# First attention of a two-layer trunk: doubled key heads, five single PSUM banks, early rows by weight, a new list order, and SyncE in that order

## The chip, the cores and the metric

The kernel runs on one core of one Trainium2 chip. A core has TensorE (PE), VectorE (DVE), ScalarE (ACT), GpSimd (POOL) and SyncE (SP); here SP only issues DMA transfers. The metric is the device time of one execution in microseconds (us), the median of several runs.

## The reference, cut to what matters

The model is a two-layer decoder trunk on 1024 rows of 1024 numbers, all in fp32. The first layer is a forgetting attention with 16 heads of 64, and the change lies in it. A gated FFN with a convolution, a shared key/value side, a sparse attention and a second FFN follow.

```python
def forgetting_attention(xn, w_in, b_f, q_gain, k_gain, w_out):
    proj = xn @ w_in
    q = rms_norm(proj[..., :HD].reshape(B, T, N_HEADS, HEAD_DIM), q_gain)
    k = rms_norm(proj[..., HD:2 * HD].reshape(B, T, N_HEADS, HEAD_DIM), k_gain)
    v = proj[..., 2 * HD:3 * HD].reshape(B, T, N_HEADS, HEAD_DIM)
    log_f = jax.nn.log_sigmoid((proj[..., 3 * HD:] + b_f).astype(jnp.float32))
    c = jnp.cumsum(log_f, axis=1).transpose(0, 2, 1)
    ...
        s = jnp.einsum('bhqd,bhkd->bhqk', qb, k) * scale
        s = s + cb[..., :, None] - c[..., None, :]
        s = jnp.where(kpos[None, :] <= qpos[:, None], s, -jnp.inf)
        p = jax.nn.softmax(s, axis=-1)
        return jnp.einsum('bhqk,bhkd->bqhd', p, v)
    ...
    return o @ w_out
```

## The kernel before, in words

Each fp32 factor is split into a high and a low part ("hi" and "lo", names ending in `_h` and `_l`), and a product is three matmuls, hi by hi, lo by hi, hi by lo (L219 to L221). ACT rounds the high part, and DVE or POOL subtracts it to get the low part.

The first layer has three stretches. `fox_in` projects q, k and v in tiles of 128 rows, row-normalizes the heads and stores q and k, transposed and split, in DRAM (`s_q`, `s_k`), and v in `s_v`. The upper eight heads of rows 512 to 1023 are left out there. `fox_attn` is the attention: in units of one head and one half of the query rows, SP loads q, k and v of the unit (L801), PE forms the scores (L626) in a pair of PSUM banks (`s`), DVE adds the mask and takes the row maximum (L634), ACT takes the exponential (L636), DVE the reciprocal (L639), and POOL scales the rows (L640). Then `key_tasks` turns the weights, one key tile at a time: PE transposes up to four 128x128 blocks into a single bank `t` (L653), ACT and DVE split them (L664 `p_h`, L666 `p_l`), and PE multiplies with v (L658, L659) into the bank `v`. Beside the attention, PE does the projections left out by `fox_in` (`late_tasks`, whose sums lie in `t` banks too) and the output projection of rows 0 to 639 (`proj_tasks`). Their weights come from DRAM in quarters of 512 KB, `w_raw<-in_a_w_in` (L706) and `w_raw<-in_a_w_out` (L928), and are split by ACT (L893 `w_h`, `wo_h`) and POOL (L894).

The order in which the queues run is made while the program is built. A `Flow` holds tasks with an engine, an assumed duration, a priority (`u` plus a number by the task's letter from a table `PLAN`) and the buffers that they take and use. It walks through the list with assumed times: on each engine, the task that could start first is emitted, and among those that could, the one of lowest priority. A task that `takes` a buffer starts only when all tasks that `use` the last tenant of its room are done. `Trunk.run` (L210) then fixes the emitted order on PE, ACT, DVE and POOL. On SP it is not fixed: there the framework's own scheduler places the DMA issues. Each queue then runs in order, and an instruction that waits holds up all behind it on that queue.

In `key_tasks` the transposes have the v buffer of their unit among the buffers that they use. The products, which read that buffer, have not:

```python
        a = F.add("PE", .109 * len(blocks) - .09, u + 1 + x, "K", turn, after=after, takes=[t, p2], uses=uses)
        ...
        rooms["uses"] = [*rooms.get("uses", ()), p2, *then_uses]
        pv.tasks.append(F.add("PE", .035 + n / 1240 + (.5 if then else 0), u + 1 + x, "V", product, after=[l, *then_after, *pv.tasks[:1]], **rooms))
```

So for the list a v buffer is free with the last transposes of its unit. In the program, the load into it waits on a semaphore for the last product. There are four v buffers.

Of the kernel before, what the change touches and what calls it, by code (L numbers as in the profile page):

```python
# [50 lines left out]
def moved(*shape):  # L51
# [4 lines left out]
PLAN = {  # L56
    "fox": dict(F=1e3, G=-11.5, R=.5, M=5, E=-1, K=-.5, H=-1.5, L=-5.5, V=2, J=-4, D=1.5, N=18.5, Q=1.5, W=13, P=-3, S=0, O=1, spread=.7, wo=.6, wo_from=21, side=2, late=2, step=1.6, gap=.015),
    "ffn0": {"": 18.5, "A": -1.5, "B": -11, "C": -11, "D": -10, "I": 4.5, "P": -12, "R": 14.5, "S": -6, "T": 23, "U": 24, "V": 23, "W": -7, "a": -2.5, "b": -12, "c": 12, "d": -7, "e": -12, "f": -4, "g": -20, "h": -8, "l": 21, "n": 16.5, "r": -8, "s": -6, "t": -6, "x": 23.5, "y": 23.5},
    "ffn1": {"": 0, "A": 12.5, "B": -4, "C": -12, "D": 12.5, "I": 15.5, "P": -11.5, "R": 3.5, "S": 12, "T": 18, "U": 24, "V": 17, "W": 4.5, "a": -12, "b": 8, "c": -12, "d": -3, "f": 0.5, "l": 19.5, "n": -11, "s": 17.5, "t": -8},
    "nin": {"": 0},  # L60
    "nsa": dict(P=20.5, S=5.0, F=23.5, G=1000.0, R=4.5, M=12.0, E=20.0, D=-12, K=1.5, H=12.0, L=-10.0, V=20.0, J=14.0, O=22, N=19.0, Q=9.5, W=16.0, spread=0.3, wo=3, wo_from=2, side=2, cmp=0.5, gap=0.05),
}
# [39 lines left out]
class Flow:  # L102
# [14 lines left out]
    def add(self, eng, dur, u, kind, fn, after=(), takes=(), uses=()):  # L117
        t = Task(eng, dur + (self.plan.get("gap", 0) if eng == "PE" else 0), u + self.plan.get(kind, 0), fn, takes, (*takes, *uses))
# [77 lines left out]
class Trunk:  # L196
# [224 lines left out]
    def fox_in(self, cp, xT, qT, kT, vS, extras, room):  # L421
        nc, A = self.nc, self.A
        w_in = A["a_w_in"][0]
        with self.pool("fi_s", 2) as sp, self.pool("fi_w", 2) as wp, \
# [12 lines left out]
            def gate():  # L437
# [37 lines left out]
                for x, c in enumerate((ch, cl)):  # L475
                    nc.sync.dma_start(kT[:, :, 2 * HD + x, :].rearrange("p a t -> (p a) t"), f32(c))

            def spill(o, dst, half, i, gain):

                tl = slice(i * P, (i + 1) * P)  # L480
                ps = pp.tile([P, 4, P], FT, name="ps_t", tag="ps_t")
                for k in range(4):
                    nc.tensor.transpose(ps[:, k], o[:, k * P:(k + 1) * P], self.ident)
                hi = sp.tile([P, 4, P], FR, name="sp_h")
                lo = sp.tile([P, 4, P], FR, name="sp_l")
                if gain is None:
                    self.split(ps, hi, lo)
                else:
                    nc.scalar.activation(hi, ps, AF.Copy, scale=gain)
                    nc.vector.scalar_tensor_tensor(lo, ps, gain, f32(hi), op0=OP.mult, op1=OP.subtract)  # L490
                for x, t in enumerate((hi, lo)):
                    for a in range(2):
                        nc.sync.dma_start(dst[4 * half:4 * half + 4, a, x * HD:(x + 1) * HD, tl].rearrange("p d t -> d p t"),
                                          f32(t[a * HD:(a + 1) * HD]))

# [82 lines left out]

    def attn_flow(self, es, tag, rooms):
# [107 lines left out]


    def fox_heads(self, p):
        self.hp = p  # L690
        self.qbs = [p.tile([66, 512], FR, name=f"qb{n}", bufs=1) for n in range(4)]
        self.loaded = 0

    def late_tasks(self, xT, weights, room, qT, kT, vS):
# [4 lines left out]
        stored = [[], [], []]  # L699
        u = plan["late"]  # L700

# [8 lines left out]
        def product(i, ws):  # L710
            ps, side = F.buf("t"), F.buf("side")
            after = []
            for k in range(ND):
# [4 lines left out]
                after = [F.add("PE", .665, u, "S" if k else "P", step, [*after, made] if made else after, [] if k else [ps, side], [w, ps, side] if k else [w])]  # L718
            return ps, side, after

# [9 lines left out]
        def heads(kind, i, ps, side, after):  # L730
# [27 lines left out]
            def store():  # L758
                for x in range(2):
                    for a in range(2):  # L760
                        nc.sync.dma_start((qT, kT)[kind][4:, a, x * HD:(x + 1) * HD, i * P:(i + 1) * P].rearrange("p d t -> d p t"),
                                          f32(hl.t[x][a * HD:(a + 1) * HD, :4]))
            return F.add("SP", moved(P, D), u, "Q", store, [a], uses=[hl])
# [7 lines left out]
        for kind in (2, 0, 1):  # L771
            ws = [there(t) for t in weights] if kind == 2 else [quarter(kind, c) for c in range(4)]
            for i in range(NT // 2, NT):
                *rooms, after = product(i, ws)
                stored[kind].append(heads(kind, i, *rooms, after) if kind < 2 else values(i, *rooms, after))
                u += plan["step"]
        return stored, after

    def fox_attn(self, qT, kT, vS, xT, weights, w_room, o_late, wo_steps, early):
        nc, hp = self.nc, self.hp  # L780
        with ExitStack() as es:
            rooms = {f"pt{r}": (2, [P, (5 + r) * P], FT, False) for r in range(4)}
            rooms.update(p2=(5, [P, 512], FR, True), ohl=(1, [P, 8, P], FR, True))
            self.attn_flow(es, "fox", rooms)
            F = self.flow
# [56 lines left out]
            for i, tiles, res, dst in early:  # L842
# [4 lines left out]
                for n, (ks, done) in enumerate(parts):  # L847
# [14 lines left out]

    def proj_tasks(self, u, wo, o, res, dst, after, late=()):


        F, nc = self.flow, self.nc
        x = F.buf("raw")
        load = F.add("SP", moved(P, D), u, "Q", lambda: nc.sync.dma_start(x.t, res), after=after[:1], takes=[x])
        sums = []
        for c in range(2):  # L870
# [6 lines left out]
            for k in range(8):  # L877
                t = F.add("PE", .665, u, "G" if k else "F", lambda k=k, f=product: f(k), after=[*after, *late] if late and k == 7 else after,
                          takes=[] if k else [ps, side], uses=[o, ps, side] if k else [o])
# [16 lines left out]

    def wo_tasks(self, steps, after=()):
        F = self.flow
        out = []
        for k, (load, room) in enumerate(steps):  # L900
            raw = F.buf("raw")
            load = F.add("SP", moved(P, D), k * F.plan["wo"] + F.plan["wo_from"], "Q", lambda f=load, b=raw: f(b.t), takes=[raw])
# [1091 lines left out]
    def nsa_attn(self, kv, q_dram, late, wo, steps, res, dst, norms, nw, many):  # L1994
# [3 lines left out]
        with ExitStack() as es:  # L1998
            self.attn_flow(es, "nsa", dict(pt0=(6, [P, T], FT, False), pt1=(5, [P, 640], FT, False), p2=(4, [P, 512], FR, True),
                                           q=(3, [P, 4, P], FR, False), c=(1, [P, 4, P], FR, True), ot=(2, [P, 2, P], FT, False)))  # L2000
            F, plan = self.flow, self.flow.plan
# [3 lines left out]
            spilled, free = late(F)  # L2005
            ready = self.wo_tasks(steps, free)

# [138 lines left out]
    def build(self, out):  # L2146
        A, nc = self.A, self.nc
        with self.pool("const", 1) as cp, self.pool("dram", 1, space=DRAM) as dp, self.pool("w", 3) as self.wp, \
                self.pool("edge", 1, side="right") as self.edge:
            qT = dp.tile([8, 2, 2 * HD, T], FT, name="s_q")  # L2150
            kT = dp.tile([8, 2, 2 * HD + 2, T], FT, name="s_k")
            vS = dp.tile([T, H, P], FT, name="s_v")
# [183 lines left out]
```

## Time and profile before

| | |
|---|---|
| median of 3 runs | 2666.33 us (2663.33 to 2669.57) |
| profiled execution | 2667.36 us |
| its span | 2665.6 us |
| PE busy | 2595.7 us, 97% |
| DVE, ACT, POOL busy | 81%, 57%, 20% |
| DMA | 310.80 MB, mean 117 GB/s |

The profiled execution is 1.0 us above the median, and 1.8 us of it lie outside the span. PE's busy time contains time at a reduced clock and short waits inside a pipelined group, so what PE loses is read from short windows: busy time and granted clock side by side.

### The profile page before, as it was taken

To read this page: it belongs to the slowest core of one execution; us is meant where nothing else is said; L and a number is where in the kernel's file an instruction comes from. 1 tells how busy PE (TensorE), PEld (TensorE's weight loads), DVE (VectorE), ACT (ScalarE), POOL (GpSimd) and SP (SyncE) were. 2 spreads that over 40 slices of the span, in tenths; PEclk is the share of its full clock that TensorE was granted. 3 is DMA by queue.
4 is the path that set the end of the run, shared out by engine and by line. 5 is a ranking of instruction groups with operands and counts; after the bars stand their busy time and mean duration, and the time that the engine had idled before them with its cause. 6 is when DMAs were issued, how large, how long until landed. Compare 5 with 4: busy or idle time off the path is not lost.

```text
span 2665.6 us, 38650 instructions
## 1 busy us (share of the span) xinstructions
PE 2595.7 (97%) x12936; PEld 2165.8 (81%) x12936; DVE 2162.6 (81%) x4471; ACT 1523.1 (57%) x3168; POOL 541.3 (20%) x846
## 2 busy tenths in 40 slices
PE   8999998899999999999999999999999999999999
PEld 6778877787888888888898788888787788888887
DVE  7762788766987877889887899889997988786988
ACT  5332777655554545444674687777876655454443
POOL 1001445420000000000354474444461000000000
PEclk9999999999999999999999999999999999999999
DMA  6474657723423222735334320001114422225553
GB/s 179 113 196 163 175 159 202 187 80 135 134 80 95 72 95 81 278 113 162 106 98 108 103 68 16 30 29 37 64 52 125 132 95 72 95 71 175 184 174 130
DMA packets 276775, 310.80 MB, mean 117 GB/s; under 512 B 19944, under 2 KB 194448, under 8 KB 276576
## 3 DMA queue, kind: packets, MB, share of 16 engines
q1 hardware_dynamic: 276144, 306.76, 37.2%
q8 instruction: 102, 1.67, 0.3%
q10 hardware_dynamic: 432, 1.57, 0.2%
q14 instruction: 97, 0.79, 0.1%
HBM read 236.84 MB, written 71.43 MB: 116 GB/s over the span
## 4 chain that ended last, share of the span: by engine, by line
PE 77%; DVE 14%; ACT 4%; issue 2%; DMA 2%; POOL 1%; SPq 0%; DVEq 0%; ACTq 0%; POOLq 0%
PE ps L220 15%; PE ps L221 15%; PE ps L219 15%; PE s L626 5%; PE t L653 5%; PE ps_m L219 3%; PE v L658 3%; PE v L659 3%; PE ps_m L221 2%; PE ps_m L220 2%; PE t L219 2%; PE t L221 2%; PE t L220 2%; DVE op L1097 2%; DVE sum L1097 1%
## 5 line engine op out<-in xcount | busy, mean ns | idle before, releaser
L1101 ACT CAST op<-sum 128x512 fp32r<-128x512 f32 x396 | 239.8, 622 | 398.8 <-PE ps L221 269.5
L219 PE MATMUL ps<-xs,op 128*128 128x512 f32 x880 | 342.7, 389 | 2.9 <-DVE u L1097 2.9
L220 PE MATMUL ps<-xs,op 128*128 128x512 f32 x880 | 342.5, 389 | 0.0
L221 PE MATMUL ps<-xs,op 128*128 128x512 f32 x880 | 342.4, 389 | 0.0
L1097 DVE TENSOR_TENSOR op<-sum,op 128x512 fp32r<-128x512 f32 x396 | 266.6, 688 | 83.1 <-ACT op L1101 82.6
L666 DVE TENSOR_TENSOR p_l<-t,p_h 128x512 fp32r<-128x512 f32 x456 | 277.8, 629 | 52.5 <-ACT p_h L664 50.4
L636 ACT ACTIVATE pt<-pt,sm 128x640 f32<-128x640 f32 (+7 forms) x384 | 287.9, 752 | 50.2 <-DVE sm L634 48.3
L664 ACT CAST p_h<-t 128x512 fp32r<-128x512 f32 x456 | 236.3, 539 | 112.1 <-PE t L653 110.2
L653 PE MATMUL t<-ident,pt 128*128 128x128 f32 x1632 | 244.6, 276 | 16.9 <-DVE p_l L666 11.7
L220 PE MATMUL ps<-op 128*128 128x512 f32 x616 | 240.2, 390 | 1.9 <-DVE op L1097 1.8
L653 PEld LDWEIGHTS t<-ident,pt 128*128 128x128 f32 x1632 | 194.7, 142 | 56.3 <-DVE p_l L666 18.0
L219 PE MATMUL ps<-op 128*128 128x512 f32 x616 | 240.2, 390 | 0.0
L221 PE MATMUL ps<-op 128*128 128x512 f32 x616 | 239.7, 389 | 0.0
L640 POOL TENSOR_SCALAR pt<-pt,sm,gate 128x640 f32<-128x640 f32 (+7 forms) x256 | 201.3, 792 | 162.6 <-DVE sm L639 127.8
L1310 DVE SCALAR_TENSOR_TENSOR acc<-u,conv,acc 128x1023 f32<-128x1023 f32 (+1 forms) x176 | 225.6, 1282 | 4.1 <-ACT acc L1311 1.3
L219 PEld LDWEIGHTS ps<-xs,op 128*128 128x128 f32 x880 | 165.2, 188 | 38.2 <-DVE u L1097 2.1
L220 PEld LDWEIGHTS ps<-xs,op 128*128 128x128 f32 x880 | 165.2, 188 | 34.6 <-DVE xs L1097 0.4
L221 PEld LDWEIGHTS ps<-xs,op 128*128 128x128 f32 x880 | 165.2, 188 | 34.4
L634 DVE CUSTOM_DVE_ANT_0 pt<-s,mask 128x128 f32<-128x128 f32 (+7 forms) x256 | 153.2, 615 | 20.4 <-PE t L653 9.3
L658 PE MATMUL v<-p_h,v 128*128 128x512 f32 (+1 forms) x376 | 154.7, 413 | 3.2 <-DVE o_early L682 1.4
L1101 ACT CAST op<-w_raw 128x512 fp32r<-128x512 f32 x132 | 81.5, 624 | 104.4 <-PE ps L221 103.5
L659 PE MATMUL v<-p_l,v 128*128 128x512 f32 (+1 forms) x376 | 139.1, 374 | 0.3 <-DVE p_l L666 0.3
(501 smaller groups left out, 6253.4 us busy)
## 6 DMA issues: line engine op xcount, KB each, us to landing
w_raw<-in_f_w_up SPq DMA_DIRECT2D x96, 512.0 KB
u<-in_f_w_down SPq DMA_DIRECT2D x176, 256.0 KB
s_g<-acc SPq DMA_DIRECT2D x40, 512.0 KB
g<-s_g SPq DMA_DIRECT2D x20, 1024.0 KB
w_raw<-in_a_w_in SPq DMA_DIRECT2D x32, 512.0 KB
qa<-s_q SPq DMA_DIRECT2D x32, 256.0 KB
ka<-s_k SPq DMA_DIRECT2D x32, 256.0 KB
v<-s_v SPq DMA_DIRECT2D x16, 512.0 KB
```

The lines of the kernel that those rows point to most:

```text
L219: mm(out, a[0], b[0], start=start, stop=False, **kw)
L220: mm(out, a[0], b[1], start=False, stop=False, **kw)
L221: mm(out, a[1], b[0], start=False, stop=stop, **kw)
L636: e = F.add("ACT", .238 + .8333e-3 * n, u, "E", lambda c=c, out=out: nc.scalar.activation(out(), out(), AF.Exp, bias=sm["nm"][:, c], scale ...
L653: nc.tensor.transpose(t.t[:, r * P:(r + 1) * P], b(), self.ident)
L658: nc.tensor.matmul(out, v(), p2.t[0][:, :n], start=first, stop=False)
L659: nc.tensor.matmul(out, v(), p2.t[1][:, :n], start=False, stop=last)
L664: h = F.add("ACT", .052 + .8333e-3 * n, u + 1 + x, "H", lambda: nc.scalar.copy(p2.t[0][:, :n], t.t[:, :n]), after=[a], uses=[t, p2])
L666: lambda: nc.vector.tensor_tensor(p2.t[1][:, :n], t.t[:, :n], f32(p2.t[0][:, :n]), op=OP.subtract), after=[h], uses=[t, p2])
L1097: TT = lambda out, a, b, op: nc.vector.tensor_tensor(out, a, b, op=op)
L1101: a = F.add("ACT", .53, u, "A", lambda: nc.scalar.copy(op.t[:, 0], src()), after, [op], uses)
L1310: return lambda: nc.vector.scalar_tensor_tensor(acc.t[:, sh:], o.t[:, :T - sh], cw[j][:, c:c + 1], acc.t[:, sh:], op0=OP.mult, op1=OP.add)
```

## The change

1. The keys are stored as hi, hi, lo and c, 194 rows for a head instead of 130, so the 128 rows of `ka` come with one transfer instead of two of 64 rows. A tile's keys are stored with six transfers instead of four (`store_pairs`).
2. The attention has five single banks `t` and one score pair `s`, instead of three and two.
3. The early rows of the output projection wait for each weight by itself (`made[k]`) and have a priority of their own (`row`). The splits of W_out wait for chosen steps of the last late product instead of its end.
4. `PLAN["fox"]` has new numbers, some now lists: one for each late tile, each W_out weight and each early row.
5. SP keeps the list's order in this attention as well.

```diff
-    "fox": dict(F=1e3, G=-11.5, R=.5, M=5, E=-1, K=-.5, H=-1.5, L=-5.5, V=2, J=-4, ...
+    "fox": dict(D=7, E=66, F=13, G=7, H=3.5, J=-12.5, K=-13.5, L=133.5, ..., V=66.5, ...
...
+        dur = dur * self.plan.get("load", 1) if eng == "SP" else dur + (self.plan.get("gap", 0) if eng == "PE" else 0)
...
-    def in_order(self):
+    def in_order(self, *more):
         e = mybir.EngineType
-        return self.tc.manual_schedule(engines={e.PE, e.Activation, e.DVE, e.Pool})
-    def run(self, flow):
-        with self.in_order():
+        return self.tc.manual_schedule(engines={e.PE, e.Activation, e.DVE, e.Pool, *more})
+    def run(self, flow, *more):
+        with self.in_order(*more):
             flow.run()
...
-                for x, t in enumerate((hi, lo)):
-                    for a in range(2):
-                        nc.sync.dma_start(dst[4 * half:4 * half + 4, a, x * HD:(x + 1) * HD, tl].rearrange("p d t -> d p t"),
-                                          f32(t[a * HD:(a + 1) * HD]))
+                self.store_pairs(dst[4 * half:4 * half + 4, :, :, tl], (hi, lo) if gain is None else (hi, hi, lo))
...
-        ring("t", 3, [P, 512], FT, space=PSUM, ordered=False)
-        ring("s", 2, [P, T], FT, space=PSUM)
+        ring("t", banks, [P, 512], FT, space=PSUM, ordered=False)
+        ring("s", (7 - banks) // 2, [P, T], FT, space=PSUM)
...
+    def store_pairs(self, dst, parts):
+        for x, t in enumerate(parts):
+            for a in range(2):
+                self.nc.sync.dma_start(dst[:, a, x * HD:(x + 1) * HD].rearrange("p d t -> d p t"), f32(t[a * HD:(a + 1) * HD]))
...
-        return stored, after
+        return stored, [steps[k:k + 1] for k in (1, 3, 5, 3, 3, 7, 7, 7)]
...
-            self.attn_flow(es, "fox", rooms)
+            self.attn_flow(es, "fox", rooms, 5)
...
-                        loaded_k = load(u, k_there, kb, *[(lambda x=x, n=n, kb=kb: kb.t[0][x * HD:(x + 1) * HD, :n], kT[p, a, :HD, :n]) for x in range(2)],
-                                        (lambda n=n, kb=kb: kb.t[1][:, :n], kT[p, a, HD:, :n]))
+                        loaded_k = load(u, k_there, kb, (lambda n=n, kb=kb: kb.t[0][:, :n], kT[p, a, :P, :n]), (lambda n=n, kb=kb: kb.t[1][:, :n], kT[p, a, P:, :n]))
...
-                self.proj_tasks(u, tiles, hl, res, dst, [*wo, ready[0]], ready[1:])
-            self.run(F)
+                self.proj_tasks(u, tiles, hl, res, dst, [ready[0]], ready[1:], [[w] for w in wo], F.plan["row"][i])
+            self.run(F, mybir.EngineType.SP)
...
-            out.append(self.split_tasks(k * F.plan["wo"] + F.plan["wo_from"], lambda n, b=raw: b.t[:, half(n)],
-                                        lambda x, n, f=room: f()[x][:, half(n)], [load, *after], [], [raw]))
+            out.append(self.split_tasks(u, lambda n, b=raw: b.t[:, half(n)],
+                                        lambda x, n, f=room: f()[x][:, half(n)], [load, *after[k]], [], [raw]))
```

The sparse attention is called with `banks` 3 and the old numbers written as a list, and its instructions, like those of both FFNs, keep their order. In the first attention the same matmuls run in another order. Two places follow.

The first is SP at the second half of the late q weights (`w_raw<-in_a_w_in`, two quarters a row). `qa`, `qb`, `ka`, `kb` and `v` are loads of a unit's factors, `s_v` is a store of late values. Before:

```order
L801 DMA qb_79<-s_q 64x512
L801 DMA ka<-s_k 64x1024 x2
L801 DMA kb<-s_k 66x1024
L801 DMA qa<-s_q 128x512
L801 DMA qb_80<-s_q 64x512
L801 DMA qb_81<-s_q 64x512
L706 DMA w_raw<-in_a_w_in 128x2x512 x2
L728 DMA s_v<-w_raw 128x1024
L706 DMA w_raw<-in_a_w_in 128x2x512 x2
L801 DMA qa<-s_q 128x512
L801 DMA ka<-s_k 64x512
L801 DMA v<-s_v 128x8x128
```

Changed:

```order
L808 DMA kb<-s_k 66x1024
L714 DMA w_raw<-in_a_w_in 128x2x512 x2
L737 DMA s_v<-w_raw 128x1024
L808 DMA qa<-s_q 128x512
L808 DMA qb_81<-s_q 64x512
L808 DMA v<-s_v 128x8x128
L808 DMA v<-s_v 128x4x128
L714 DMA w_raw<-in_a_w_in 128x2x512 x2
L808 DMA qa<-s_q 128x512
L808 DMA qb_78<-s_q 64x512
```

The second pair of quarters has moved behind two v loads. These are the first of the attention that go into a v buffer in use, and the second of them waits for the last product (L660) of the unit that held it.

On ACT, the split of the third quarter (`w_h<-w_raw`, two halves) stands in the changed kernel like this among exponentials (L637) and the copies `p_h` of turned weights (L665):

```order
L637 ACTIVATE pt_3024,sm<-pt_3024,sm 128x896
L900 CAST w_h<-w_raw 128x512 x2
L665 CAST p_h<-t 128x512
L637 ACTIVATE pt_3060,sm<-pt_3060,sm 128x1024
L665 CAST p_h<-t 128x384
```

Behind the split stands a `p_h` which empties a bank. On PE, the last product of that v buffer's unit and what follows it in the changed kernel:

```order
L654 MATMUL t<-ident,pt_2931 128x128
L659 MATMUL v<-p_h,v 128x256
L660 MATMUL v<-p_l,v 128x256
L627 MATMUL s<-ka,qa 128x128
L627 MATMUL s<-kb,qb_80 128x128
L627 MATMUL s<-ka,qa 128x256
L627 MATMUL s<-kb,qb_80 128x256
L659 MATMUL v<-p_h,v 128x128
L660 MATMUL v<-p_l,v 128x128
L654 MATMUL t<-ident,pt_2931 128x128
L223 MATMUL t<-w_h,wo_h 128x512
L224 MATMUL t<-w_l,wo_h 128x512
```

The second L660 row is the product that the v load waits for; the transposes of the row behind it take the bank that the `p_h` above must have emptied.

The second place is SP at the weights of the output projection (`w_raw<-in_a_w_out`). Before:

```order
L761 DMA s_k<-ohl_h 64x4x128 x2
L761 DMA s_k<-ohl_l 64x4x128 x2
L801 DMA v<-s_v 128x4x128
L928 DMA w_raw<-in_a_w_out 128x1024
L761 DMA s_k<-ohl_h 64x4x128 x2
L761 DMA s_k<-ohl_l 64x4x128 x2
L928 DMA w_raw<-in_a_w_out 128x1024 x2
L801 DMA qa<-s_q 128x512
```

Changed:

```order
L808 DMA v<-s_v 128x8x128
L936 DMA w_raw<-in_a_w_out 128x1024
L808 DMA v<-s_v 128x8x128
L694 DMA s_k<-ohl_h 64x4x128 x4
L694 DMA s_k<-ohl_l 64x4x128 x2
L936 DMA w_raw<-in_a_w_out 128x1024
L808 DMA qa<-s_q 128x512
L808 DMA qb_80<-s_q 64x512
L808 DMA ka<-s_k 128x1024
L808 DMA kb<-s_k 66x1024
```

Each weight now stands right behind a v load, one of them also behind the six stores of a late tile's keys; eight rows further down another weight follows another v load.

More of the change, by code (lines that the diff above doesn't have):

```diff
@@ L56 @@
 PLAN = {
-    "fox": dict(F=1e3, G=-11.5, R=.5, M=5, E=-1, K=-.5, H=-1.5, L=-5.5, V=2, J=-4, D=1.5, N=18.5, Q=1.5, W=13, P=-3, S=0, O=1, spread=.7, wo=.6, wo_from=21, side=2, late=2, step=1.6, gap=.015),
+    "fox": dict(D=7, E=66, F=13, G=7, H=3.5, J=-12.5, K=-13.5, L=133.5, M=-20, N=-4, P=5.5, Q=17, R=-15, S=32.5, V=66.5, W=15.5, none=3,
+                late=[-42.8, -9.6, -12, -3.4, 23.8, 55.8, 82.6, 105.2, 41.8, 101.4, 108.4, 133.4],
+                wo=[185.6, 15.4, 125.4, 177.6, 186.8, 162.4, 145.8, 146], row=[57, -51, -24, -206, 196.5],
+                spread=.7, side=2, gap=.015, load=1.2),
     "ffn0": {"": 18.5, "A": -1.5, "B": -11, "C": -11, "D": -10, "I": 4.5, "P": -12, "R": 14.5, "S": -6, "T": 23, "U": 24, "V": 23, "W": -7, "a": -2.5, "b": -12, "c": 12, "d": -7, "e": -12, "f": -4, "g": -20, "h": -8, "l": 21, "n": 16.5, "r": -8, "s": -6, "t": -6, "x": 23.5, "y": 23.5},
@@ L117, in add @@
     def add(self, eng, dur, u, kind, fn, after=(), takes=(), uses=()):
-        t = Task(eng, dur + (self.plan.get("gap", 0) if eng == "PE" else 0), u + self.plan.get(kind, 0), fn, takes, (*takes, *uses))
+        dur = dur * self.plan.get("load", 1) if eng == "SP" else dur + (self.plan.get("gap", 0) if eng == "PE" else 0)
+        t = Task(eng, dur, u + self.plan.get(kind, 0), fn, takes, (*takes, *uses))
         t.side = kind in "FG"
@@ L574, in head_norm, with attn_flow @@
         nc.vector.tensor_tensor(o, ps, r[:, :, None].to_broadcast([P, n, HD]), op=OP.mult)
-    def attn_flow(self, es, tag, rooms):
+    def attn_flow(self, es, tag, rooms, banks):
         en = es.enter_context
@@ L699, in late_tasks @@
         stored = [[], [], []]
-        u = plan["late"]
+        order = iter(plan["late"])
+        u = next(order)
         def quarter(kind, c):
@@ L711, in product @@
             ps, side = F.buf("t"), F.buf("side")
-            after = []
+            after, steps = [], []
             for k in range(ND):
@@ L758, in store @@
             def store():
[L759 to L762, printed above, removed]
+                self.store_pairs((qT, kT)[kind][4:, :, :, i * P:(i + 1) * P], [hl.t[x][:, :4] for x in ((0, 1), (0, 0, 1))[kind]])
             return F.add("SP", moved(P, D), u, "Q", store, [a], uses=[hl])
@@ L773, in late_tasks @@
             for i in range(NT // 2, NT):
-                *rooms, after = product(i, ws)
+                *rooms, steps = product(i, ws)
+                after = steps[-1:]
                 stored[kind].append(heads(kind, i, *rooms, after) if kind < 2 else values(i, *rooms, after))
-                u += plan["step"]
-        return stored, after
+                u = next(order, 0)
+        return stored, [steps[k:k + 1] for k in (1, 3, 5, 3, 3, 7, 7, 7)]
     def fox_attn(self, qT, kT, vS, xT, weights, w_room, o_late, wo_steps, early):
@@ L861, in raw_ring, with proj_tasks @@
         self.flow.ring("raw", lambda: self.wraw([P, D]), 3)
-    def proj_tasks(self, u, wo, o, res, dst, after, late=()):
+    def proj_tasks(self, u, wo, o, res, dst, after, late=(), made=None, shift=0):
         F, nc = self.flow, self.nc
+        made = made or [()] * 8
         x = F.buf("raw")
@@ L877, in proj_tasks @@
             for k in range(8):
-                t = F.add("PE", .665, u, "G" if k else "F", lambda k=k, f=product: f(k), after=[*after, *late] if late and k == 7 else after,
+                t = F.add("PE", .665, u + shift, "G" if k else "F", lambda k=k, f=product: f(k), after=[*after, *made[k], *(late if k == 7 else ())],
                           takes=[] if k else [ps, side], uses=[o, ps, side] if k else [o])
@@ L895, in split_tasks, with wo_tasks @@
             after, takes, uses)
-    def wo_tasks(self, steps, after=()):
+    def wo_tasks(self, steps, after):
         F = self.flow
@@ L901, in wo_tasks @@
             raw = F.buf("raw")
-            load = F.add("SP", moved(P, D), k * F.plan["wo"] + F.plan["wo_from"], "Q", lambda f=load, b=raw: f(b.t), takes=[raw])
+            u = F.plan["wo"][k]
+            load = F.add("SP", moved(P, D), u, "Q", lambda f=load, b=raw: f(b.t), takes=[raw])
             half = lambda n: slice(n * 512, (n + 1) * 512)
-            out.append(self.split_tasks(k * F.plan["wo"] + F.plan["wo_from"], lambda n, b=raw: b.t[:, half(n)],
-                                        lambda x, n, f=room: f()[x][:, half(n)], [load, *after], [], [raw]))
+            out.append(self.split_tasks(u, lambda n, b=raw: b.t[:, half(n)],
+                                        lambda x, n, f=room: f()[x][:, half(n)], [load, *after[k]], [], [raw]))
         return out
@@ L2005, in nsa_attn @@
             spilled, free = late(F)
-            ready = self.wo_tasks(steps, free)
+            ready = self.wo_tasks(steps, [free] * 8)
             def scores(i, br, qb):
@@ L2150, in build @@
             qT = dp.tile([8, 2, 2 * HD, T], FT, name="s_q")
-            kT = dp.tile([8, 2, 2 * HD + 2, T], FT, name="s_k")
+            kT = dp.tile([8, 2, 3 * HD + 2, T], FT, name="s_k")
             vS = dp.tile([T, H, P], FT, name="s_v")
```

9 lines of the change are left out of this document (5 added, 4 removed).

## The prediction

> **What bounds the kernel now.** I read the engine table first, then the windows over the three stretches of the program, then ten-microsecond windows inside the first attention, then the chain of waits at the worst of them, then the waits of SP and PE.
>
> ```profile
> PE 2595.7 (97%) x12936; PEld 2165.8 (81%) x12936; DVE 2162.6 (81%) x4471; ACT 1523.1 (57%) x3168; POOL 541.3 (20%) x846
> ```
>
> PE is the bound. The change leaves PE's work as it is: the same matmuls, in another order, in the first attention alone. So it can only win or lose what PE loses there. The windows give start and end, length, then busy time of PE, PEld, DVE, ACT and POOL, the granted clock, the DMA share and GB/s: the projections, the attention, and all the rest.
>
> ```profile
> 0.00:254.80 254.80, 241.82 (x1114) 191.94 (x1115) 153.65 (x368) 92.25 (x184) 12.18 (x16) 0.99 0.59 160
> 254.80:617.60 362.80, 339.31 (x1883) 287.33 (x1883) 266.26 (x705) 243.06 (x564) 138.06 (x160) 0.98 0.57 162
> 617.60:2665.00 2047.40, 2014.60 (x9941) 1686.53 (x9939) 1742.69 (x3398) 1187.83 (x2420) 391.05 (x670) 1.00 0.32 103
> ```
>
> In the attention PE is idle for 362.8 - 339.3 = 23.5 us. Where:
>
> ```profile
> 300.00:310.00 10.00, 8.14 (x39) 7.05 (x38) 6.48 (x22) 6.98 (x19) 5.54 (x7) 0.83 0.69 245
> 430.00:440.00 10.00, 6.46 (x40) 5.11 (x38) 9.42 (x24) 9.21 (x23) 6.51 (x7) 1.00 0.73 212
> 440.00:450.00 10.00, 7.40 (x39) 6.17 (x40) 8.53 (x21) 6.98 (x16) 4.54 (x7) 0.83 0.69 196
> 460.00:470.00 10.00, 7.73 (x42) 6.75 (x40) 6.37 (x24) 8.91 (x23) 9.35 (x11) 0.83 1.02 278
> 470.00:480.00 10.00, 4.43 (x26) 3.53 (x27) 3.47 (x7) 3.76 (x8) 2.53 (x2) 0.94 1.02 225
> 480.00:490.00 10.00, 8.87 (x39) 7.74 (x40) 7.91 (x21) 7.01 (x17) 5.20 (x5) 0.72 0.38 126
> ```
>
> The idle parts of these six add up to 1.86 + 3.54 + 2.60 + 2.27 + 5.57 + 1.13 = 17.0 us, most of the 23.5. The clock column adds to it: 0.17 + 0.17 + 0.17 + 0.06 + 0.28 = 0.85 of 10 us, 8.5 us at full speed. Together 25.5 us. The chain shows what they are (start, duration, what), here the first and the second stall.
>
> ```profile
> 295.24 6.84 DMA w_raw<-in_a_w_in
> ...
> 302.63 0.61 ACT w_h L893
> 303.25 0.38 ACT p_h L664
> 303.66 0.57 DVE p_l L666
> 304.36 1.47 PE t L653 x7
> ...
> 309.93 0.23 PE t L220
> ...
> 428.98 0.22 PE t L653 x2
> ...
> 431.44 0.13 PE v L659
> 431.58 0.38 SPq L801
> 432.01 0.57 SPq L801
> 432.69 6.77 DMA w_raw<-in_a_w_out
> 439.48 0.63 ACT wo_h L893
> 440.17 1.28 POOL wo_l L894
> 441.51 1.09 PE t L653 x4
> ...
> 465.32 12.67 DMA w_raw<-in_a_w_out
> 478.53 0.59 ACT p_h L664
> ```
>
> Each time ACT stands at a weight split whose 512 KB are not there, the copies `p_h` behind the split wait too, no bank `t` is emptied, and PE has no room for the next transposes. At 431.44 the chain goes back to a product with v (PE, L659): SP was held by a v load until that product was done, and the weight's issue stood behind it. SP's waits in the attention say how much of this there is.
>
> ```profile
> SPq L801 <- PE v L659: 65.0, 14, 14.1
> SPq L761 <- ACT p_h L664: 17.1, 3, 10.9
> PE t L653 <- DVE p_l L666: 9.8, 7, 5.5
> PE s L626 <- DVE sm L634: 2.6, 5, 1.1
> ```
>
> SP waits 65.0 us for products of v in 14 waits. The next row is SP waiting to store late keys. PE's largest visible wait is for a bank, and its wait for a score pair is 2.6 us.
>
> **The change, part by part.** (1) Doubled keys. A pair of stores and a pair of 64-row loads cost SP:
>
> ```profile
> 135.49 1.23 SPq L493 DMA_DIRECT2D s_k<-sp_h  x2
> 290.57 1.23 SPq L801 DMA_DIRECT2D ka<-s_k  x2
> 10.79 3.92 DMA w_raw<-in_a_w_in
> ```
>
> Sixteen tiles store two more transfers each, 32 x 0.62 (half of a row's 1.23) = 20 us of SP, and 32 x 128 KB = 4.2 MB; 24 `ka` loads fewer inside the attention take 24 x 0.62 = 15 us off. The bytes loaded are the same. While nothing waits behind them these cost nothing, their cover being PE's 254.8 us of projections for 24 of the stores. Uncovered are the weights of `fox_in` that now stand about one tile later on SP, after more stores: in the order PE has 4.5 to 7.5 us of matmuls between the release of such a load and its first use, 11 to 15 before. Against the 3.92 us landing at 10.79, two splits and the issue of up to two stores, that just about holds. I take 1.5 us; ends 0 and 4 (one landing fully exposed).
>
> (2) Banks and score pair. Five banks let transposes run on when `p_h` is late, one score pair makes a score block wait until DVE has read the one before. The gain is bounded by the idle time outside the six windows, 23.5 - 17.0 = 6.5 us. The loss: 96 score blocks with some 339.3 / 96 = 3.5 us of PE between them, while DVE needs for the widest block 1.21 us (below). In the changed list 8 of the 96 stand too close for that, by about 1 us each. I take a gain of 5 us net, since the nearest row (2.6 us in 5 waits, with two pairs) is small; ends -6.5 and +8.
>
> (3) and (4) Waits by weight and new numbers. They fix no duration. They set where loads and splits stand, which is part (5).
>
> (5) SP in the list's order. This is the term that decides. The list takes a v buffer to be free with the unit's last transposes. The new numbers put transposes early (K = -13.5) and products late (V = 66.5), so the product that the v load in truth waits for can be 10 us further on. SP holds at that load, and the weight, which the list wanted earlier, stands behind it. Before, the framework placed SP's rows, and there was 5 to 17 us of PE work between a weight's release and the first transposes that hang on it. I counted this in the changed order with 0.23 us for a 512-wide matmul and 0.11 for a transpose (the chain's rows at 309.93 and 428.98). Where a weight follows a v load it is: 0.0 us at the third quarter of the late q weights, 0.7 at the last quarter of the late k weights, then at three W_out weights 4.8, 4.5 and 6.4. At one more v load, with the six key stores behind it, 6.1.
>
> The price of the whole chain from the weight's issue to PE: 304.36 - 295.24 = 9.1 us in the first stall. With 0.38 us for the v load ahead it is 9.5. With the 3.92 us landing in place of 6.84 it is 6.6. I take 8.0, between them, because the new places have two or three transfers of 256 to 512 KB in flight, as the first stall has, but not the three that made 12.67. What else lies in the chain comes from these groups:
>
> ```profile
> L634 DVE CUSTOM_DVE_ANT_0 pt<-s,mask 128x1024 f32<-128x1024 f32 x16 | 19.4, 1210 | 0.5 <-PE t L653 0.4
> L636 ACT ACTIVATE pt<-pt,sm 128x640 f32<-128x640 f32 x16 | 13.4, 837 | 6.4 <-DVE sm L634 6.4
> ```
>
> - Third late q quarter: 8.0 - 0.0 = 8.0 us.
> - Last late k quarter: 8.0 - 0.7 = 7.3.
> - First of the three W_out weights: a 1024-wide mask pass lies in the chain, 8.0 + 1.2 - 4.8 = 4.4.
> - Second: six key stores lie ahead, 6 x 0.62 = 3.7, and the stall before it runs meanwhile: 8.0 + 3.7 - 4.5 - 4.4 = 2.8.
> - Third: an exponential of 0.84 and a row cast of about that length stand ahead of `p_h` on ACT, with a second split: 8.0 + 2.0 - 6.4 = 3.6.
> - The v load with six stores: no weight, but the buffer of the late tile comes free later: 8.0 - 6.1, rounded up for the stores, 2.2.
>
> Sum 28.3 us of idle PE; with 6.6 or 9.5 for the chain about 20 or 37. The clock comes on top. Before, five windows lost 8.5 us, 1.7 each; six places make 10.2. In all 38.5 us against the 25.5 that go: +13.0.
>
> The rule of the Trainium skill, "TensorE: Matmul & The Clock Gate", "Part 1: The HAM clock gate", is that the half clock comes after at least one idle window of about 3.4 us. By it only the first two places would lose clock, 3.4 us by the row's 1.7 each, and the sum would be 6.8 us lower. The trace does not agree with so long an idle window: the window at 300 has 1.86 us of idle in all and a clock of 0.83.
>
> **The sum.** +1.5 - 5.0 + 13.0 = +9.5 us on 2667.36, which is 2676.9. The profiled execution was 1.0 above the median of 2666.33, so I forecast a median of 2676.
>
> **Rivals.** (a) Faster. The price of a chain at these places is at its low end or under it, because SP gets to the v load after the product is long done, held before that by another wait. Then the queue is what the list meant it to be: the two largest places fall to about 2 us each, the idle sum is 28.3 - 11.3 = 17.0, four places lose clock (6.8), in all 23.8 against 25.5, and with the full bank gain of 6.5 and `fox_in` at 0 the profiled time is 8.2 lower, the median 2658. If the W_out places fall too, their 13 us go as well: 2645. For it: five `t` banks hold more turned weights, and SP's 65.0 us of waits for products before did not all reach PE. Against it: at the third quarter no matmul at all lies between release and need, so anything that SP does adds. It decides when the landing with its splits is under 5 us at both places.
>
> (b) No change. The stalls change place and sum to the same 25.5: the chain price is 6.6 at all places (sum 20 + 8.5 for the clock, 28.5), the banks give 5, `fox_in` takes 1.5: 2666. For it: both kernels have the same weights to fetch, and DMA is busy to 0.57 in both.
>
> (c) The single score pair becomes the bound. A wait in the row of 2.6 us in 5 is 0.52 us. If each of the 96 score blocks waits half of that, it is 24 us instead of a gain of 5, and 13.0 + 1.5 + 24 makes 2705; with only the 8 close blocks at 1 us it is 2689. For it: DVE is busy for 266 of 363 us. Against it: 3.5 us of other PE work between blocks.
>
> (d) The keys' longer stores reach the path. Of 32 stores, 8 lie in the attention, 8 x 0.62 = 5 us on SP's already held queue: 2681. "DMA: Bandwidth & Descriptors", "Rules for kernel authors", in the Trainium skill says that two transfers to disjoint halves of the partitions gain nothing by being apart, since they share the same engines; by that the merged `ka` load saves SP's issue time alone, the 15 us above, and lands no sooner. No row here shows it.
>
> **How the numbers follow.** The forecast (slower by 5 to 17 us) has 0.40, (a) 0.27, (b) 0.19, (c) 0.08, (d) 0.06. What a measurement of this kernel tells from no change is about 0.2%, 5.3 us: faster is below 2661.0, slower above 2671.7. Faster comes from (a), 0.27. Within are (b) and a part of the forecast's low end, 0.22. Slower is the rest, 0.51. The range leaves out the far ends of (a), below 2653, and of (c), above 2692. The forecast's own range is 2671 to 2684.
>
> **What would show it.** In the changed kernel's chain of waits there should be, some 40 us and again some 120 us of PE time into the attention, a piece PE `v` L660, then SP L808, then `w_raw<-in_a_w_in`, ACT `w_h` L900, `p_h` L665, and PE `t` L654, with PE idle 7 to 8 us in it. Between them PE should have less idle time than before outside such places. SP's waits for PE `v` should be over 65 us. The wait of PE `s` for DVE should stay below 8 us; (c) would show as 20 and more. If the idle time of PE in the attention is at 20 us or less, the first two places have not come, and (a) is right. If the windows before the first score are 4 us longer, `fox_in` was undersized.

## The result, and the profile after

The changed kernel takes 2695.79 us (median of 4 runs, 2694.92 to 2696.99) against 2667.95 for the kernel before in the same comparison: a ratio of 1.0115, 95% interval 1.0102 to 1.0128. It is 27.8 us slower. The sign was forecast, and the 2676 of the forecast and its upper end of 2692 were both too low.

The engine table of the changed kernel and its windows over the same three stretches (start and end, length, busy PE, PEld, DVE, ACT, POOL, granted clock, DMA share, GB/s):

```profile
PE 2604.0 (97%) x12936; PEld 2174.7 (81%) x12936; DVE 2161.5 (80%) x4471; ACT 1521.3 (56%) x3168; POOL 539.3 (20%) x846
```

```profile
0.00:268.10 268.10, 247.50 (x1117) 194.82 (x1118) 154.88 (x369) 92.59 (x185) 12.20 (x16) 0.98 0.57 157
268.10:641.80 373.70, 340.58 (x1875) 292.14 (x1875) 261.91 (x704) 241.12 (x563) 136.57 (x160) 0.95 0.53 163
641.80:2693.00 2051.20, 2015.88 (x9947) 1687.78 (x9945) 1744.68 (x3400) 1187.62 (x2420) 390.55 (x670) 1.00 0.32 103
```

The instruction counts of the five engines are the same. The loss has three parts. I cut the trace of each profiled execution (2667.36 us before, 2695.40 changed) at the first score matmul and at the last matmul of the early output projection, which gives "projections", "attention" and "rest":

| kernel | projections | attention | rest |
|---|---|---|---|
| before | 254.8 | 363.7 | 2047.1 |
| changed | 268.1 | 373.6 | 2051.8 |
| difference | +13.3 | +9.9 | +4.7 |

**The attention.** The two large stalls are where the forecast put them. Windows, and the chain of waits of the changed kernel at the first:

```profile
310.00:320.00 10.00, 2.79 (x13) 2.27 (x12) 2.66 (x9) 4.51 (x10) 3.61 (x3) 0.65 0.68 212
400.00:410.00 10.00, 2.63 (x11) 1.96 (x10) 2.15 (x9) 4.22 (x10) 3.57 (x3) 0.75 0.72 210
```

```profile
310.52 0.12 PE v L660
...
310.67 0.37 SPq L808
...
311.17 4.25 DMA w_raw<-in_a_w_in
...
315.96 0.61 ACT w_h L900
316.58 0.49 ACT p_h L665
...
317.10 0.70 DVE p_l L667
...
317.84 0.48 PE t L654
```

PE ends the product at 310.64, SP issues the v load and then the weight, the weight lands, ACT splits it, `p_h` and `p_l` empty a bank, and PE goes on at 317.84: 7.2 us with nothing else to do (forecast: 8.0). At 400.3 the same happens with the last quarter of the late k weights; PE idles from 401.1 to 408.4, 7.4 us (forecast: 7.3). Rows of the timeline show it (in brackets the idle time of the engine before the row, and what ended it):

```profile
400.83 0.45 SPq L714 DMA_DIRECT2D w_raw<-in_a_w_in  x1
405.73 1.14 ACT L900 CAST wo_h<-w_raw 128x512 fp32r<-128x512 f32 x2 [8.71 <-DMA w_raw<-in_a_w_in]
407.28 0.56 DVE L667 TENSOR_TENSOR p_l<-t,p_h 128x384 fp32r<-128x384 f32 x1 [8.73 <-ACT p_h L665]
408.44 0.69 PE L627 MATMUL s<-ka,qa 128*128 128x384 f32 x1 [7.37 <-DVE sm L635]
```

ACT waits for the weight, DVE for a `p_h` behind the weight's split, and the mask pass that PE waits for stands behind that on DVE. The third large stall was not listed as such:

```profile
486.36 1.47 SPq L694
...
490.61 0.55 SPq L936
...
491.20 1.29 SPq L808
...
493.70 8.14 DMA kb<-s_k
```

Here SP goes through the six stores of a late tile's keys, a W_out weight and other loads until the keys of the next unit have their turn, and the last of these, `kb`, takes 8.14 us to land with all that in flight. PE waits 4.9 us for `ka`. What SP and PE wait for:

```profile
SPq L808 <- PE t L654: 84.5, 20, 11.0
SPq L808 <- PE v L660: 68.0, 16, 9.8
PE s L627 <- DVE sm L635: 14.9, 9, 7.4
PE t L654 <- DVE p_l L667: 7.2, 1, 7.2
PE s L627 <- DMA ka<-s_k: 4.9, 1, 4.9
```

SP's wait for products (68.0 us) is hardly larger than before (65.0). What changed is what stands behind it. Of the 14.9 us that PE waits for a score pair, 7.4 is the second stall. In the windows of the attention PE's idle time rises from 23.5 to 373.7 - 340.6 = 33.1 us, and its busy time by 1.3: the loss there is idle time.

**The projections.** Here PE stalls where it did not before, at 157 to 166 us and at 188 to 193. The window over the first place, ACT's row for the first of the late weights (start, duration, and in brackets the idle time before it and its releaser), and the chain at both:

```profile
150.00:170.00 20.00, 16.51 (x67) 11.60 (x65) 10.91 (x24) 7.25 (x13) 0.00 (x0) 0.91 0.81 214
```

```profile
155.91 1.05 ACT L229 CAST w_h<-w_raw 128x1024 fp32r<-128x1024 f32 x1 [0.85 <-DMA w_raw<-in_a_w_in]
```

```profile
157.24 0.60 ACT qk_o L571
157.84 0.94 ACT w_h L229
158.79 0.68 DVE hn_ss L573
159.47 1.14 DVE w_l L230
160.66 0.50 PE ps_m L224
...
166.47 0.43 PE ps_m L224
...
189.90 0.26 SPq L694
190.20 0.62 SPq L694
190.92 1.95 DMA col_in<-in_kc_pe
193.46 0.70 PE ps_m L223
```

At 157 the weights of the next block come too late to be split ahead of their use: ACT takes them behind a head's norm (`qk_o`), DVE behind another, and PE waits for both. At 188 PE waits for a small column load, `col_in`, that stands on SP behind the six stores of a key tile. By the windows, PE's idle time in the projections rises from 13.0 to 20.6 us, 7.6 of the 13.3; the rest is busy time that has grown by 5.7, and the clock is 0.91 at 150 to 170 and at 180 to 200 us, where it was 1.00 before.

**Behind the attention.** PE waits 3.4 us for rows that go out to DRAM and come back:

```profile
643.16 0.61 DVE w_raw L890
643.79 6.77 DMA s_h<-w_raw
650.58 3.67 DMA h_rows<-s_h
```

The last early row is stored only when its sum has come, and its store takes 6.77 us. SP waits 6.4 us for it; in the kernel before it waited 2.3, and PE's longest wait for these rows was 1.1. The window with PE's wait, in the changed kernel, also shows a lower clock, where the kernel before has 1.00 (636 to 646 us):

```profile
655.00:665.00 10.00, 6.68 (x28) 5.79 (x29) 6.76 (x15) 7.29 (x21) 1.12 (x1) 0.83 0.29 108
```

The longer wait, 2.3 us, and the clock, 0.17 of 10 us, make 4.0 of the 4.7.

### The profile page after: what moved, and what is told of

Its sections match the earlier page's. It is cut to its first block, busy times and chain, and to the rows that moved or that the text cites. A ratio compares the mean times of both kernels' runs of the same rounds, so it can differ in the third digit from the quotient of the medians.

```text
span 2693.6 us, 38618 instructions
## 1 busy us (share of the span) xinstructions
PE 2604.0 (97%) x12936; PEld 2174.7 (81%) x12936; DVE 2161.5 (80%) x4471; ACT 1521.3 (56%) x3168; POOL 539.3 (20%) x846
## 4 chain that ended last, share of the span: by engine, by line
PE 78%; DVE 14%; ACT 3%; DMA 2%; issue 2%; SPq 1%; POOL 0%; DVEq 0%; ACTq 0%; POOLq 0%
PE ps L224 15%; PE ps L223 15%; PE ps L225 15%; PE s L627 6%; PE t L654 6%; PE v L660 3%; PE v L659 3%; PE ps_m L224 3%; PE ps_m L223 3%; PE ps_m L225 3%; PE t L223 2%; PE t L225 2%; PE t L224 2%; DVE op L1105 2%; DVE sum L1105 2%
## 5 line engine op out<-in xcount | busy, mean ns | idle before, releaser
L637 ACT ACTIVATE pt<-pt,sm 128x640 f32<-128x640 f32 (+7 forms) x384 | 288.2, 753 | 56.1 <-DVE sm L635 54.6
L665 ACT CAST p_h<-t 128x512 fp32r<-128x512 f32 x456 | 233.4, 541 | 102.8 <-PE t L654 99.8
L660 PE MATMUL v<-p_l,v 128*128 128x512 f32 (+1 forms) x376 | 138.4, 375 | 4.0 <-DVE p_l L667 4.0
```

The source lines that it names most:

```text
L637: e = F.add("ACT", .238 + .8333e-3 * n, u, "E", lambda c=c, out=out: nc.scalar.activation(out(), out(), AF.Exp, bias=sm["nm"][:, c], scale ...
L660: nc.tensor.matmul(out, v(), p2.t[1][:, :n], start=False, stop=last)
L665: h = F.add("ACT", .052 + .8333e-3 * n, u + 1 + x, "H", lambda: nc.scalar.copy(p2.t[0][:, :n], t.t[:, :n]), after=[a], uses=[t, p2])
```

## The experiments

Each time is compared with the kernel before on the same chip. In the table at the end of this section the three stretches are those of the profiled execution.

**1. The doubled keys alone, on the kernel before.**

```diff
+                self.store_pairs(dst[...], (hi, lo) if gain is None else (hi, hi, lo))
...
+                        loaded_k = load(u, k_there, kb, (... kb.t[0][:, :n], kT[p, a, :P, :n]), (... kT[p, a, P:, :n]))
```

> The kernel before with the doubled keys alone: six stores a key tile, one ka load; banks, list numbers and SP's freedom as before. Theory (three separate losses: projections 13.3 us by the stores, attention 10 us by SP's kept order, 4 us behind it): the first score comes at 267 to 269 us instead of 254.9, and the time is about 2668 + 13 = 2681, with the attention near its 363.7 us. Rival (the loss in the projections comes from SP being kept in order, or from the list): first score at 255 to 257 and 2667 to 2670.

Measured 2675.63 against 2663.40, ratio 1.0046 (1.0029 to 1.0064): 12.2 us slower, and the first score at 267.6. The loss in the projections comes with the keys, whatever the list and SP do in the attention. The attention itself is 3.4 us shorter, which says little: the list assumes other load times here, so that some of its rows stand in another order.

**2. The changed kernel without them.**

```diff
-                self.store_pairs(dst[...], (hi, lo) if gain is None else (hi, hi, lo))
+                self.store_pairs(dst[...], (hi, lo))
...
+                        loaded_k = load(..., *[two loads of 64 rows], ..., took=moved(P, n) + moved(66, n))
```

> The changed kernel without the doubled keys: four stores a key tile, two ka loads, while the list assumes the same load time, so that PE, ACT, DVE and POOL keep the changed order in the attention. Theory: first score back at 255, time 2696 - 13 = 2683, the two stalls of 7 us in the attention still there. Rival: first score still at 268 and about 2695.

Measured 2677.82, ratio 1.0051 (1.0032 to 1.0070), first score at 256.4, and the two stalls are still there (PE waits 7.5 and 6.9 us). The projections' loss is gone, from the other side.

**3. The changed kernel with SP free in the attention.**

```diff
-            self.run(F, mybir.EngineType.SP)
+            self.run(F)
```

> The changed kernel with SP's order in the attention left to the framework again; every other queue has the same rows in the same order. The weights then no longer stand behind v loads in use (8 to 16 us of PE work between release and need instead of 0.0 and 0.7). Theory: both 7 us stalls and the three after them shrink, the attention falls from 373.7 to 350 to 358 us, the time to 2672 to 2680, while the first score stays at 268. Rival (the single score pair and the new list are what costs): the attention stays above 368 us and the time at 2690 to 2696.

Measured 2663.38 against 2663.40, ratio 0.9996 (0.9986 to 1.0007). The first score stays at 266.3, and the attention falls to 337.2 us, more than expected. PE, ACT, DVE and POOL have the rows of the changed kernel in the same order. By the traces, keeping SP in the list's order costs 373.6 - 337.2 = 36.4 us, and the new list with its banks, with SP free, saves 363.7 - 337.2 = 26.5. But this kernel's profiled execution, 2655.16, is the fastest of ten, 8.2 us below their median, with the highest clock of them (0.997 over the whole execution; seven of the ten have 0.993 or 0.994). By the medians SP's order costs 28 us: the changed kernel is 27.8 slower than the one before, this one is level with it. The lower clock, 0.003 to 0.004 of 2660 us, is of the size of these 8 us; in which stretch the others lose it isn't shown. SP's waits in this kernel's attention, and its window:

```profile
SPq L808 <- PE v L660: 23.2, 15, 3.6
```

```profile
266.30:603.50 337.20, 327.01 (x1875) 281.21 (x1874) 260.31 (x704) 240.38 (x563) 136.16 (x160) 1.00 0.57 174
```

The same products hold SP for 23.2 us instead of 68.0, since other issues go first, and the clock is at 1.00.

**4. The kernel before with SP kept.**

```diff
-            self.run(F)
+            self.run(F, mybir.EngineType.SP)
```

> The kernel before with SP kept in the list's order in the attention, and nothing else. One W_out weight then has 0.4 us of PE work between its v load's release and its need, two late quarters 5.6 and one 7.0, instead of 5 and more, 14.5 and 15.7. Theory (a kept SP order that does not know of the products costs with any list): 2668 + 8 to 14 = 2676 to 2682. Rival (the old list's order of loads is good, and only the new numbers make it bad): 2665 to 2670.

Measured 2685.21, ratio 1.0080 (1.0064 to 1.0097): 21.8 us slower, above the expected 8 to 14. The attention takes 380.6 us, 16.9 more. SP's waits for products of v double:

```profile
SPq L801 <- PE v L659: 126.8, 17, 13.8
```

So a kept order on SP costs with the old numbers too. The rival, that only the new numbers make it bad, is out.

**5. Single keys and SP free, with the new banks and numbers.** Experiments 2 and 3 in one kernel.

> The changed kernel without the doubled keys and with SP left to the framework in the attention; banks, list and the other queues as changed. Theory (the two losses add and have nothing to do with each other): first score at 255 to 257, attention 337 to 343 us, the rest some 2050, so 2644 to 2650, a ratio of 0.991 to 0.994 to the kernel before. Rival (the gain of the free order hangs on the single ka load): attention over 350 us, 2657 and more.

Measured 2646.87 against 2665.74, ratio 0.9928 (0.9913 to 0.9943), first score 256.3, attention 336.9. It is faster than both kernels. It was timed again beside experiment 10, as experiment 11, and gave 2649.05, ratio 0.9941 (0.9928 to 0.9954). The losses add, to within 3 to 5 us: taking off 13.4 (experiment 2) and 28 (experiment 3) would leave 14 us of gain, and it is 18.9 and 16.4. The profiled execution lies at the median here, so these are the better figures for the attention: against experiment 2, whose engines have the same rows in the same order, SP's freedom saves 366.9 - 336.9 = 30.0 us, and against the kernel before the list and its banks save 363.7 - 336.9 = 26.8.

> The free-SP kernel with single keys again, beside the one with the later row tile 4 on the same chip: 2644 to 2650 us, a ratio of 0.991 to 0.994 to the kernel before.

**6. The second copy of the keys stored by another queue.** Bytes and layout as in the changed kernel.

```diff
+                q = self.nc.gpsimd if side and x == 1 and len(parts) == 3 else self.nc.sync
+                q.dma_start(dst[:, a, x * HD:(x + 1) * HD].rearrange("p d t -> d p t"), ...)
```

> The changed kernel, with the second copy of the keys' high part in the projections stored by GpSimd's queue instead of SP's: the same bytes and the same layout, but four stores a key tile on SP. The weights then stand on SP where they stood before. Theory (the loss of 13 us is the place of the weights in SP's queue): first score at 255 to 258, time about 2696 - 11 = 2685. Rival (the 3 MB more of stores in the projections slow the weights' transfers): first score at 265 to 269 and about 2695.

Measured 2683.51, ratio 1.0066 (1.0051 to 1.0081), first score at 255.6. The bytes alone cost less than 1 us there. SP's issues of the next block's weights show what does: in the kernel before, in the changed one, and in this one.

```profile
138.43 1.84 SPq L352 DMA_DIRECT2D w_raw<-in_a_w_in  x2
```

```profile
142.43 2.56 SPq L694 DMA_DIRECT2D s_k<-sp_h  x4
145.09 1.24 SPq L694 DMA_DIRECT2D s_k<-sp_l  x2
...
148.70 1.24 SPq L694 DMA_DIRECT2D s_q<-sp_h  x2
150.04 1.24 SPq L694 DMA_DIRECT2D s_q<-sp_l  x2
...
152.32 0.90 SPq L356 DMA_DIRECT2D w_raw<-in_a_w_in  x2
```

```profile
139.15 1.64 SPq L356 DMA_DIRECT2D w_raw<-in_a_w_in  x2
```

With six stores a tile on SP the framework's scheduler put the weights behind the next two tiles, 13.9 us later. With four they stand where they stood, 0.7 us off.

**7. The list told when a v buffer comes free.** SP kept, numbers as changed.

```diff
-        rooms["uses"] = [*rooms.get("uses", ()), p2, *then_uses]
+        rooms["uses"] = [*rooms.get("uses", ()), p2, *then_uses, *[b for b in uses if b.ring is F.rings.get("v4")]]
```

> The changed kernel, with the products named among the tasks that use a v buffer, so that the list knows when it comes free; SP kept, all numbers as changed. The weights have at least 4.7 us of PE work between release and need. Theory (SP's kept order costs because the list has the wrong release): no stall of 7 us is left, the attention is at 340 to 355 us, the time 2662 to 2678. Rival (keeping SP costs whatever the list knows): attention over 365 us, 2687 and more.

Measured 2677.10, ratio 1.0042 (1.0027 to 1.0057), attention 353.1, no stall of 7 us. It lies at the upper edge of what was expected. Of the attention's 373.6 us, 20.5 go, and it is still some 16 above experiments 3 and 5; by the medians 16.4 of the 28 us go. What is left of PE's waits in this attention is mostly the score pair:

```profile
PE s L627 <- DVE sm L635: 10.4, 12, 1.5
```

The edit also makes a new list, so what the known release does and what the other order does can't be told apart fully.

**8. Three banks and two pairs with the new numbers, SP free.**

```diff
-            self.attn_flow(es, "fox", rooms, 5)
+            self.attn_flow(es, "fox", rooms, 3)
```

> The changed kernel with SP free in the attention and with three banks and two score pairs again, the list made anew with the same numbers. It tells whether the 26 us that the attention gained with SP free came with the banks or with the numbers. Theory (five banks are what lets transposes run on while a p_h is late): attention 350 to 365 us, time 2675 to 2690. Rival (the numbers do it): attention 335 to 345 us and 2661 to 2670.

Measured 2726.58, ratio 1.0232 (1.0215 to 1.0249), attention 401.6: 64.4 us more than with five banks, far above the expected 350 to 365.

**9. Five banks and one pair with the old numbers, SP free, keys once.**

```diff
-        ring("t", 3, [P, 512], FT, space=PSUM, ordered=False)
-        ring("s", 2, [P, T], FT, space=PSUM)
+        ring("t", 5 if tag == "fox" else 3, [P, 512], FT, space=PSUM, ordered=False)
+        ring("s", 1 if tag == "fox" else 2, [P, T], FT, space=PSUM)
```

> The kernel before with five single banks and one score pair in the first attention, the list made anew with the old numbers; keys once and SP free as before. It tells whether the banks alone bring the gain. Theory (banks and numbers go together: three banks with the new numbers took 401.6 us): no gain, attention 360 to 385 us, time 2662 to 2690. Rival (five banks are the gain with any numbers): attention 335 to 350 us, time 2640 to 2655.

Measured 2703.09, ratio 1.0141 (1.0127 to 1.0156), attention 390.4: as expected no gain, and a little more loss than the range. Here the single pair is a bound, as rival (c) had it:

```profile
PE s L626 <- DVE sm L634: 27.7, 32, 1.4
```

Neither the banks nor the numbers gain alone (experiment 8 also has the waits by weight and the doubled keys). Together, with SP free, they gain 26.8 us of the attention (experiment 5).

**10. Row tile 4 taken back later behind the attention**, in the kernel of experiment 5.

```diff
-            h = row()
-            nc.sync.dma_start(h, h_dram[4])
-            ahead(4, h)
             for i in range(done, NT):
                 h = tile(i, o)
+                if i == done:
+                    h4 = row()
+                    nc.sync.dma_start(h4, h_dram[4])
+                    ahead(4, h4)
```

> The free-SP kernel with single keys, in which the stage behind the attention takes row tile 4 back from DRAM after its first own tile instead of ahead of it, so that some 10 us of matmuls cover its store and load. Theory (the 4 us behind the attention are the wait of PE for that round trip): the rest falls from 2051.8 to 2047 to 2049 us and the time by 3 to 4 us against the same kernel without it. Rival (the loss is the order of DVE there, or another wait comes in its place): no change beyond 1 us.

Measured 2648.03, ratio 0.9938 (0.9923 to 0.9954), beside 2649.05 for the kernel without the edit: no difference, and the rest at 2053.5 against 2053.7. But the edit did not do its work. In its trace the row still goes out and comes back at the same place (chain of waits), and PE still waits 3.1 us for it, 3.5 in experiment 11:

```profile
595.89 6.71 DMA s_h<-w_raw
...
602.62 3.42 DMA h_rows<-s_h
```

So it says nothing on the cause. The 4 us behind the attention stay open.

| kernel | projections | attention | rest |
|---|---|---|---|
| 1 before, keys doubled | 267.6 | 360.3 | 2047.8 |
| 2 changed, keys once | 256.4 | 366.9 | 2053.6 |
| 3 changed, SP free | 266.3 | 337.2 | 2049.8 |
| 4 before, SP kept | 255.1 | 380.6 | 2047.6 |
| 5 keys once, SP free | 256.3 | 336.9 | 2051.8 |
| 6 changed, stores on another queue | 255.6 | 372.5 | 2051.0 |
| 7 changed, v known | 268.0 | 353.1 | 2053.6 |
| 8 changed, SP free, 3 banks | 268.5 | 401.6 | 2053.1 |
| 9 before, 5 banks | 254.6 | 390.4 | 2057.2 |

## Why the prediction was right in sign and wrong in size

**Part (1), the doubled keys: the step that failed.** I saw that the weights of `fox_in` came later on SP (I took one tile; it was two), set the 4.5 to 7.5 us of PE work left against a landing of 3.92 us, two splits and the issue of two stores, found that this "just about holds" and took 1.5 us, with 4 as the upper end. It was 13.3. The landing was about right: the weights issued at 152.32 were there at 155.91. I counted the splits, 0.94 us on ACT and 1.14 on DVE in the chain, but not that they wait their turn: both stood behind the norms of a head, which themselves wait for PE. Nor did I count a slower clock there. And I priced only the weights: every row behind the six stores moved, also the column load that cost PE 4.1 us at 188. That the stores' place in SP's queue is the cause, and not their bytes, is shown by experiments 1, 2 and 6.

**Part (5), SP in the list's order: right in its mechanism.** The mechanism, the two places and their price came out (7.2 and 7.4 us against 8.0 and 7.3). The whole of it is 28 us by the medians, 30.0 by the traces of experiments 2 and 5, 36.4 by those of the changed kernel and experiment 3; my sum, 28.3 idle and 10.2 clock, was 38.5, too large. Even in the last pair its split is off: PE is idle 33.1 - 10.2 = 22.9 us more with SP kept, and busy 340.6 - 327.0 = 13.6 more. In experiment 7, where the list knows the release of a v buffer, more than half of the loss is gone, though the list is new there too. One of the smaller places was misread: I priced a W_out weight with 2.8 us where the keys of the next unit were what PE waited for, 4.9.

**Parts (2) to (4): right by netting.** The 25.5 us that were to go and the 5 us for the banks make 30.5; experiments 3 and 5 show 26.5 and 26.8. This and the sum of part (5) were both too large, and the errors cancel. I gave the first to the stalls' disappearance and the second to the banks. Experiments 8 and 9 show that they can't be given to either: the banks lose 26.7 us without the numbers, the numbers 37.9 without the banks. The net of the attention was forecast at +8.0 and is +9.9; that it comes so close is in part luck.

**The rest: not seen.** +4.7 us behind the attention had no term. It goes with the new list: the two kernels with the old list and three banks, experiments 1 and 4, have 2047.8 and 2047.6, those with another list 2049.8 to 2057.2. The chain names the store of the last early row, and PE's wait for it with the clock behind it covers 4.0 us; why the store takes so long, and that it is the cause, is argued, not shown.

**The rivals.** (a) is out: SP was not held by something else at the two places. (b) is out. (c) did not come in the changed kernel, whose score waits outside the second stall are 7.5 us, but it came in experiment 9. (d), longer stores on the path, was the nearest to the truth, but in the wrong stretch: I looked for it in the attention, with 8 stores, and dismissed it for the projections, where the 24 others lie.

**The clock.** I took 1.7 us of lost clock for each stall. The loss can begin with short gaps: at 157 to 166 us PE has three, of 1.05, 1.62 and 0.76 us, and the matmul behind them at 166.47 takes 0.43 us and not 0.23; the window around them has 3.49 us of idle PE and a clock of 0.91. But the length of a gap does not decide. Experiment 3 has gaps of 1.05, 1.62 and 0.77 us at the same place and a clock of 1.00, and the kernel before has one of 1.96 at 369 with a clock of 1.00 around it:

```profile
164.15 0.50 PE L223 MATMUL ps_m<-w_h,xT 128*128 128x512 f32 x1 [1.62 <-ACT w_h L229]
```

```profile
150.00:170.00 20.00, 16.50 (x74) 11.93 (x73) 12.08 (x29) 8.21 (x16) 0.00 (x0) 1.00 0.82 213
```

```profile
365.00:375.00 10.00, 7.33 (x43) 5.97 (x42) 9.80 (x25) 6.64 (x17) 5.28 (x6) 1.00 0.70 213
```

These are a gap of the changed kernel, the window of experiment 3 and that of the kernel before. So a fixed price for each stall is too simple, and part of the projections' loss can differ from execution to execution. What decides is not shown. The Trainium skill, "TensorE: Matmul & The Clock Gate", "Part 1: The HAM clock gate", asks for an idle window of about 3.4 us. By the first stall of 7.2 us, with a clock of 0.65 in its ten microseconds, the trace agrees; by the gaps at 157 to 166 us, the longest of them 1.62, it does not.

**The queue.** The Trainium skill, "DMA: Bandwidth & Descriptors", "Anatomy of one DMA — SWDGE (gpsimd) path", says that a wait on a semaphore happens on the issuing sequencer, ahead of dispatch. The section describes transfers that GpSimd issues; the trace agrees for SP: its v issue at 310.67 follows the product's end by 0.03 us, and the weight's issue follows that. What stands behind such a wait waits too, and that cost 28 to 36 us here.

## What to carry to other kernels

Where a queue of DMA issues is kept in a planner's order, the planner must know the releases that the program waits for: one load whose buffer is freed later than the list thinks holds up every load behind it, and the loss appears on an engine three steps away. Before such an order is kept, leave that queue to the scheduler and compare: here the gain of the list and its banks, 26.8 us of the attention, was hidden behind it. And two more stores a tile are not free because the queue has idle time; look at which loads now stand behind them, and price the whole chain from landing to the engine that waits.

## What the runs showed of the hardware

In the chains shown, a weight of 512 KB in the first attention landed in 4.25 to 12.67 us, and one load of 264 KB in 8.14. One issue of a key store in the projections held SP for 0.62 to 0.64 us, so six of them hold the queue for 3.8 us (2.56 and 1.24). A lower clock (0.91 over 20 us) followed PE gaps of at most 1.62 us at 157 to 166 us of the changed kernel; it did not follow such gaps in experiment 3, nor one of 1.96 us in the kernel before.
